# A decoder trunk on one core: the second down pair's parts behind named roundings, and thirteen second-pass pairs by seven products with six of their units kept as whole forms

## The chip, the cores and the metric

The kernel runs on one core of a Trainium2 chip. The metric is the device time of one execution in microseconds. The core has a matmul engine (TensorE, PE in the profile, its weight loads PEld), a vector engine (VectorE, DVE), a scalar engine (ScalarE, ACT), a general engine (GpSimd, POOL) and a queue engine (SyncE, SP). Each engine works through its own list in order. Transfers between the chip's memory (DRAM) and the working memory are issued on SP's or POOL's queue and carried out by 16 DMA engines.

## The reference

The reference is a trunk of two layers on 256 tokens of width 2048, all in 32-bit floats. With the attention cut down to its call, a layer is

```python
for l in range(DEPTH):                                  # DEPTH = 2
    h = _rmsnorm(x, attn_norm_g[l])
    q, k, v, gate_b, gate_c, conv_in = jnp.split(h @ w_in[l], splits, axis=-1)
    ...                                                 # differential attention; short convolution
    x = x + jnp.concatenate([attn, conv], axis=-1) @ w_out[l]
    hm = _rmsnorm(x, mlp_norm_g[l]) @ w_up[l]           # 2048 -> 8192
    x = x + jnp.square(jax.nn.relu(hm)) @ w_down[l]     # 8192 -> 2048
```

The change lies in the last two lines, the MLP.

## The kernel before

**Two parts for each number.** TensorE multiplies a rounded 32-bit form. To keep the precision, each operand is split into a high part (ScalarE copies it into the rounded form) and a low part (VectorE subtracts the high part from the original, and rounds the rest). A product is then three matmuls, high by high, high by low and low by high (`TERMS`). So each weight that is loaded costs ScalarE one pass and VectorE one pass before TensorE may use it. `halves`, `column` and `parts` do this for the different weights.

**The MLP's stages.** The 8192 hidden values are taken as 32 pairs of 128 (`NP`). A pair's up projection gives a tile `h` of blocks A11, A12, A21, A22, each 128 by 128: two halves of the hidden pair by two halves of the tokens. The down projection of a pair is thus a product of a 2 by 2 grid of blocks with a 2 by 2 grid of weight blocks of 128 by 512. There are two ways to do it:

- plain: eight block products, 24 matmuls (line 1142 in the second pass). The weights of a pair are loaded as 1 MB (`raw`) and rounded in two steps of 128 by 1024 (`rows`, line 308).
- by seven products, the scheme of Strassen and Winograd, 21 matmuls (`product`, line 983). It needs sums of the blocks on both sides. On the hidden side these are S1 to S4 (`square`, lines 960 to 963). On the weights' side `quarters` makes three groups of forms: `plain` (the blocks b1 and b2, rounded), `sums` (the tile t of differences, its first half rounded as t13) and `more` (t's second half, rounded as t24). The buffers of b2 and t13 are single; b1 and t24 have two; t has one.

**First pass.** For each pair i TensorE does the up projection (line 937) and, `LAG` = 2 pairs behind, the seven products of pair i - 2 with the left half of the output columns. The rounded form of the pair (`f`, made by `rounded`, two buffers) is used for that. The last two pairs go plain (line 1062). Every pair is also stored in DRAM for the second pass: a pair that is plain there as its rounded form (`plain`, line 969), a pair that goes by seven products there as the unrounded `h` with its sums, 448 KB (`hid`, line 965).

**Second pass.** The same pairs times the right half of the columns. `SEVEN` names the pairs that go by seven products. Such a pair's unit is loaded again into a tile `h` on SP's queue (`load_again`) and rounded again (`unit`, line 975, 128 by 896). Plain pairs come back as blocks of two (`block`, POOL's queue, four buffers). After the last pair of `SEVEN` its products are added into the output (`shared`); after the last plain pair come the rest, and in layer 1 the stores.

**What sets the order.** TensorE's list is in the order of the program. The lists of the other engines are laid out by a planner, which simulates the program's timeline when the kernel is built and may take an instruction earlier than the program names it. Three helpers bind it: `late(ins)` keeps an instruction in program order, `behind(a, b)` lets what is issued within it come only after the given instructions on their engines, and a priority block moves instructions ahead. Weights are made up to `AHEAD` = 3 jobs ahead of TensorE's use, in a list (`weights.order`) that `mlp` writes out; in the second pass the jobs of a seven-product pair are spread among the jobs of the plain pairs before it.

The first down pairs of a layer are a special case. Pair 0's three groups of forms are made during the out projection, behind the roundings that `EARLY_FORMS` names. Pair 1's groups are kept in program order (`keep = late if i == 1`), so they come where TensorE's list reaches them. From pair 2 on the planner places them. `ahead.splits` is the list of the out projection's roundings, one ScalarE and one VectorE instruction each. `split_gained` rounds the normalized activations in the same two steps (lines 275 and 276); `Norm.chunk` calls it for each quarter of the width.

Of the kernel before, what the change touches and what calls it, by code (L numbers as in the profile page):

```python
# [9 lines left out]
F32 = mybir.dt.float32  # L10
F32R = mybir.dt.float32r
AF = mybir.ActivationFunctionType
ALU = mybir.AluOpType
AX = mybir.AxisListType

P = 128
DEPTH = 2
D = 2048
S = 256
# [11 lines left out]
KG = 4  # L31
# [1 line left out]
AHEAD = 3  # L33
NP = DFF // (2 * P)
LAG = 2
SEVEN = (4, 6, 8, 11, 13, 15, 17, 19, 22, 24, 26, 28)
PLAIN = tuple(i for i in range(NP) if i not in SEVEN)

OUT_JOBS = D // P // 2 * (D // CH)
# [68 lines left out]
def trunk(ctx: ExitStack, tc: tile.TileContext, x, w_in, w_out, conv_w, q_norm_g, k_norm_g,  # L108
          lambda_q1, lambda_k1, lambda_q2, lambda_k2, subln_g, attn_norm_g, mlp_norm_g,
          w_up, w_down, rel_bias, selector, out):  # L110
    nc = tc.nc
# [7 lines left out]
    dram = ctx.enter_context(tc.tile_pool(name="dram", bufs=1, space=bass.MemoryType.DRAM))  # L119
# [8 lines left out]
    def behind(*instructions):  # L128

        stack = ExitStack()  # L130
        for ins in instructions:
            stack.enter_context(tc.issue_after(ins.ins))
        return stack

    def bank(name):
        return ps.tile([P, CH], F32, tag="bank", name=name)
# [43 lines left out]
    def norm_gain(which, l, k):  # L180
        i = l * (D // P) + k
        return gains[:, MG + i:MG + i + 1] if which else ngains[:, i:i + 1]
# [89 lines left out]

    def split_gained(dst, k, src, gain, keep=lambda ins: None):

        keep(nc.scalar.activation(dst[:, 0, k], src, AF.Copy, scale=gain))
        keep(nc.vector.scalar_tensor_tensor(
            dst[:, 1, k], src, gain, dst[:, 0, k].bitcast(F32), op0=ALU.mult, op1=ALU.subtract))

    class Parts:

# [158 lines left out]
    class Norm:  # L439
# [9 lines left out]
        def chunk(self, n, wait, banks=None):  # L449
            yield wait  # L450
            a = self.tiles[n].open()
            for j in range(2):
                tp = banks[j] if banks else bank(f"tpn{n}_{j}")
                for i in range(2):
                    k = 2 * j + i
                    for t in range(NT):
                        nc.tensor.transpose(
                            tp[:, i * S + t * P:i * S + (t + 1) * P],
                            xs[n][:, t, k * P:(k + 1) * P], ident)
                with tc.high_priority() if self.which and n == D // CH - 1 else ExitStack():  # L460
                    for i in range(2):
                        k = 2 * j + i
                        split_gained(a, k, tp[:, i * S:(i + 1) * S],
                                     norm_gain(self.which, self.l, n * KG + k))
                self.tiles[n].ready = 2 * j + 2
            self.squares(n)

# [290 lines left out]
    def mlp(l, mnorm, ahead, last):  # L758
# [3 lines left out]
        with ExitStack() as scope:  # L762
            upool = scope.enter_context(tc.tile_pool(name="upool", bufs=3))
            fpool = scope.enter_context(tc.tile_pool(name="fpool", bufs=2))
# [4 lines left out]
            def tile_of(tag, shape, dtype, *rooms):  # L769
                n = turn[tag] = turn.get(tag, -1) + 1  # L770
                pool, tag_in = rooms[max(n - (tag == "draw"), 0) % len(rooms)]
                return pool.tile(shape, dtype, tag=tag_in, name=tag, bufs=1)
# [37 lines left out]
            def quarters(i, col=0):  # L810


                keep = late if i == (SEVEN[0] if col else 1) else lambda ins: None

                def parts(src, tag, bufs):
                    hi, lo = (tile_of(tag + p, list(src.shape), F32R,
                                      *((r, tag + p) for r in (first, second)[:bufs]))
                              for p in "hl")
                    keep(nc.scalar.activation(hi, src, AF.Copy))  # L819
                    keep(nc.vector.tensor_sub(lo, src, hi.bitcast(F32)))  # L820
                    return hi, lo

                def plain():
                    raw = forms["raw"] = load_rows(i, col).rearrange("p k (n c) -> p k n c", n=2)
                    h1, l1 = parts(raw[:, 0, 0], "b1", 2)
                    h2, l2 = parts(raw[:, 1], "b2", 1)
                    return (h1, l1), (h2[:, 0], l2[:, 0]), (h2[:, 1], l2[:, 1])

                def sums():
                    raw = forms["raw"]  # L830
                    t = forms["t"] = first.tile([P, 4, CH], F32, tag="t", name="t")

                    keep(nc.vector.tensor_sub(t[:, 0:2], raw[:, :, 1], raw[:, 0]))  # L833
                    h, lw = parts(t[:, 0:2], "t13", 1)

                    keep(nc.vector.tensor_add(t[:, 2], t[:, 1], raw[:, 0, 0]))
                    keep(nc.vector.tensor_sub(t[:, 3], raw[:, 1, 0], t[:, 2]))  # L837
                    return (h[:, 0], lw[:, 0]), (h[:, 1], lw[:, 1])

                def more():  # L840
                    h, lw = parts(forms["t"][:, 2:4], "t24", 2)
                    return (h[:, 0], lw[:, 0]), (h[:, 1], lw[:, 1])

                if i == 0 and col == 0:
                    made = []
                    for make, job in zip((plain, sums, more), EARLY_FORMS):
                        with behind(*ahead.splits[job - OUT_JOBS]):
                            made.append(make())
                    return tuple(lambda n=n: made[n] for n in range(3))
                return plain, sums, more  # L850

            def rows(i, k, box, col=0):
# [19 lines left out]
            for i in range(NP - LAG, NP):  # L872
# [3 lines left out]

            hid = {i: dram.tile([P, 7 * P], F32, name=f"hid{l}_{i}") for i in SEVEN}
            plain = [dram.tile([P, 2, 2, 4, P], F32R, name=f"plain{l}_{b}")  # L880
                     for b in range(len(PLAIN) // 2)]
            again = {}

            def load_again(i):
                again[i] = tile_of("h", [P, 8, P], F32, (fpool, "h"), (second, "h"))
                nc.sync.dma_start(again[i][:, 1:].rearrange("p a c -> p (a c)"), hid[i])

            def unit(i):
                def make():
                    f = rounded(again[i], 1, 8)  # L890
                    later = SEVEN.index(i) + 1
                    if later < len(SEVEN):
                        load_again(SEVEN[later])
                    return f
                return make
# [54 lines left out]
            def square(i, h):  # L950


                u = h[:, 0:4].rearrange("p a c -> p (a c)")
                nc.scalar.activation(u, u, AF.Relu)
                top = h[:, 0:4].rearrange("p (k t) c -> p k t c", t=2)[:, :, 0]
                nc.vector.tensor_mul(top, top,
                                     mnorm.ratio.unsqueeze(1).to_broadcast([P, 2, P]))
                nc.scalar.activation(u, u, AF.Square)
                if i < NP - LAG:
                    nc.vector.tensor_add(h[:, S1], h[:, A21], h[:, A22])  # L960
                    nc.vector.tensor_sub(h[:, S2], h[:, S1], h[:, A11])
                    nc.vector.tensor_sub(h[:, S3], h[:, A11], h[:, A21])
                    nc.vector.tensor_sub(h[:, S4], h[:, A12], h[:, S2])
                if i in hid:
                    nc.gpsimd.dma_start(hid[i], h[:, 1:].rearrange("p a c -> p (a c)"))
                    return rounded(h, 1, 8)
                f = rounded(h, 0, 8 if i < NP - LAG else 4)
                b = PLAIN.index(i)
                stored.append(nc.gpsimd.dma_start(plain[b // 2][:, b % 2], f[:, :, :4]))
                return f  # L970

            def rounded(h, lo, hi):
                f = fpool.tile([P, 2, 8, P], F32R, tag="f", name="f")
                nc.scalar.activation(f[:, 0, lo:hi], h[:, lo:hi], AF.Copy)  # L974
                nc.vector.tensor_sub(f[:, 1, lo:hi], h[:, lo:hi], f[:, 0, lo:hi].bitcast(F32))  # L975
                return f
# [10 lines left out]
            for i in range(NP):  # L987
                j = i - LAG
                end = i == NP - 1
                h = tile_of("h", [P, 8, P], F32, (fpool, "h"), (second, "h"))  # L990
# [39 lines left out]

            def block(b):
                blocks[b] = apool.tile([P, 2, 2, 4, P], F32R, tag="a", name="g")
                for s in range(2):
                    nc.gpsimd.dma_start(blocks[b][:, s], plain[b][:, s])

            block(0)

            def onto(dst, p, base):
# [15 lines left out]
            sums = shared(*left)  # L1054

            prods[8] = ps.tile([P, CH], F32, tag="av", name=f"pr{l}8", bufs=1)
            for j in range(NP - LAG, NP):
                for k in range(2):
                    b = weights.take()
# [25 lines left out]
            for i in range(NP):  # L1085
                if i in SEVEN:
                    f = weights.take()
# [26 lines left out]
                b, slot = divmod(PLAIN.index(i), 2)  # L1114
# [7 lines left out]
                if i == PLAIN[-1]:  # L1122
                    both = [weights.take() for k in range(2)]
# [34 lines left out]
    for l in range(DEPTH):  # L1158
        mnorm, ahead = mixer(l, norm, first_loads if l == 0 else lambda weights: None)
# [33 lines left out]
```

## Time and profile before

| | |
|---|---|
| median of 3 runs | 2151.32 us (2151.31 to 2152.33) |
| the profiled execution, its own time | 2150.28 us |
| its span, first to last instruction | 2148.5 us |
| granted TensorE clock, mean | 0.999 |
| TensorE busy | 2132.9 us, 10962 matmuls |
| VectorE busy | 1691.0 us |
| ScalarE busy | 1300.1 us |
| DMA | 477.05 MB |

In the profiled execution layer 0's first pass runs from about 393 to 912 us and its second pass to 1081 us; layer 1's first pass from about 1461 to 1978 us and its second pass to the end. A row of the profile names the line, the engine, what is written from what, and the shape; `upc` is the up projection's bank, `pr` the banks of the first pass's products, `rt` those of the second pass, `g` a block of plain pairs, `draw` and `raw` the weights as loaded. A busy TensorE is not TensorE at its peak, since the matmuls overlap; the distance from the start of one matmul to the start of the next is the better measure of its pace.

### The profile page before, as it was taken

What the parts mean: (1) busy time and instruction counts of PE and PEld (TensorE: products, weight loads), DVE (VectorE), ACT (ScalarE), POOL (GpSimd) and SP (SyncE); (2) the same over time, 40 slices, a digit from 0 to 9 for tenths busy, and PEclk for the clock granted to TensorE, in tenths of its full rate; (3) what the DMA queues carried; (4) which work ended last, traced back from release to release, by engine and by line L of the source; (5) the groups of instructions that cost most, each with busy time, mean ns of one, the idle gap of its engine ahead of it and who ended that gap; (6) DMA issues with size and microseconds to landing.
All of it is one profiled execution on the core that took longest, in us unless ns stands there. A gap on an engine that the chain in (4) does not pass through costs nothing.

```text
span 2148.5 us, 28991 instructions
## 1 busy us (share of the span) xinstructions
PE 2132.9 (99%) x10962; PEld 1811.2 (84%) x10962; DVE 1691.0 (79%) x2307; ACT 1300.1 (61%) x1767; POOL 166.0 (8%) x253
## 2 busy tenths in 40 slices
PE   9999999999999999999999999999999999999999
PEld 7888888878888888888888888888788888888887
DVE  6667656688888888799766776566988888887996
ACT  6556445566666666656565664455666666665563
POOL 1021200000000000100001221000000000001000
PEclk9999999999999999999999999999999999999999
DMA  7655668567777777798456556675777777778982
GB/s 257 186 159 165 185 206 264 178 217 230 225 231 234 225 233 225 250 367 308 167 175 177 157 167 186 218 243 187 234 227 231 226 230 233 226 231 277 366 304 76
DMA packets 288245, 477.05 MB, mean 222 GB/s; under 512 B 10689, under 2 KB 191592, under 8 KB 288104
## 3 DMA queue, kind: packets, MB, share of 16 engines
q1 hardware_dynamic: 268104, 417.73, 61.6%
q0 software_dynamic: 19680, 57.18, 8.1%
q8 instruction: 86, 1.41, 0.3%
q14 instruction: 55, 0.45, 0.1%
q10 hardware_dynamic: 320, 0.28, 0.0%
HBM read 441.04 MB, written 34.10 MB: 221 GB/s over the span
## 4 chain that ended last, share of the span: by engine, by line
PE 95%; DVE 3%; ACT 1%; issue 1%; DMA 0%; POOL 0%; SPq 0%; DVEq 0%; ACTq 0%
PE upc L937 31%; PE pr L983 13%; PE rt L1142 9%; PE o L392 8%; PE rt L983 5%; PE ci L414 4%; PE gc L414 4%; PE gb L414 4%; PE v L392 4%; PE q L392 4%; PE k L392 3%; PE upw L937 1%; PE up L937 1%; PE pr L1062 1%; DVE wlo L308 1%
## 5 line engine op out<-in xcount | busy, mean ns | idle before, releaser
L308 DVE TENSOR_TENSOR wlo<-raw,whi 128x1024 fp32r<-128x1024 f32 x328 | 403.4, 1231 | 244.8 <-ACT whi L307 239.4
L307 ACT ACTIVATE whi<-raw 128x1024 fp32r<-128x1024 f32 x328 | 347.0, 1059 | 409.0 <-PE rt L1142 82.7
L937 PE MATMUL upc<-nT,uhi 128*128 128x512 f32 x1920 | 479.0, 392 | 0.0
L795 ACT ACTIVATE uhi<-uraw 128x1024 fp32r<-128x1024 f32 x256 | 270.5, 1057 | 261.7 <-PE upc L937 231.2
L796 DVE TENSOR_TENSOR ulo<-uraw,uhi 128x1024 fp32r<-128x1024 f32 x256 | 313.3, 1224 | 125.7 <-ACT uhi L795 114.6
L937 PEld LDWEIGHTS upc<-nT,uhi 128*128 128x128 f32 x1920 | 353.6, 189 | 68.6
L937 PEld LDWEIGHTS upc<-nT,ulo 128*128 128x128 f32 x1920 | 262.2, 191 | 18.8
L937 PE MATMUL upc<-nT,ulo 128*128 128x256 f32 x1920 | 267.8, 282 | 0.0
L1142 PE MATMUL rt<-whi,g 128*128 128x512 f32 x608 | 191.9, 389 | 0.0
L392 PE MATMUL o<-whi,cat 128*128 128x512 f32 x512 | 159.5, 390 | 0.0
L1142 PEld LDWEIGHTS rt<-whi,g 128*128 128x128 f32 x608 | 114.1, 188 | 23.4
L1142 PE MATMUL rt<-wlo,g 128*128 128x512 f32 x304 | 118.7, 391 | 0.3 <-DVE wlo L308 0.3
L392 PEld LDWEIGHTS o<-whi,cat 128*128 128x128 f32 x512 | 96.2, 188 | 19.7
L820 DVE TENSOR_TENSOR t13l<-t,t13h 128x1024 fp32r<-128x1024 f32 x84 | 102.8, 1223 | 2.1
L820 DVE TENSOR_TENSOR t24l<-t,t24h 128x1024 fp32r<-128x1024 f32 x84 | 102.5, 1221 | 2.2 <-ACT t24h L819 2.2
L819 ACT ACTIVATE t24h<-t 128x1024 fp32r<-128x1024 f32 x84 | 88.7, 1055 | 24.4 <-DVE t L837 24.4
L820 DVE TENSOR_TENSOR b2l<-draw,b2h 128x1024 fp32r<-128x1024 f32 x84 | 102.5, 1220 | 0.5 <-ACT b2h L819 0.5
L833 DVE TENSOR_TENSOR t<-draw 128x1024 f32<-128x1024 f32 x84 | 102.5, 1220 | 0.1
L975 DVE TENSOR_TENSOR f<-h,f 128x896 fp32r<-128x896 f32 (+2 forms) x88 | 98.8, 1123 | 2.5 <-ACT f L974 2.4
L392 PE MATMUL o<-wlo,cat 128*128 128x512 f32 x256 | 99.6, 389 | 0.0
L983 PE MATMUL pr<-t13h,f 128*128 128x512 f32 x240 | 94.0, 392 | 1.6 <-ACT t13h L819 1.6
L819 ACT ACTIVATE t13h<-t 128x1024 fp32r<-128x1024 f32 x84 | 89.1, 1060 | 8.4 <-DVE t L833 3.7
(357 smaller groups left out, 3834.7 us busy)
## 6 DMA issues: line engine op xcount, KB each, us to landing
uraw<-in_w_up_dram SPq DMA_DIRECT2D x128, 1024.0 KB, 5.9
raw<-in_w_in_dram SPq DMA_DIRECT2D x190, 512.0 KB, 4.2
draw<-in_w_down_dram SPq DMA_DIRECT2D x88, 1024.0 KB, 6.0
raw<-in_w_down_dram SPq DMA_DIRECT2D x40, 1024.0 KB, 13.3
raw<-in_w_out_dram SPq DMA_DIRECT2D x64, 512.0 KB, 4.9
plain<-f POOLq DMA_DIRECT2D x40, 512.0 KB, 3.8
g<-plain POOLq DMA_DIRECT2D x40, 512.0 KB, 9.3
hid<-h POOLq DMA_DIRECT2D x24, 448.0 KB, 6.2
```

What stands on the lines that cost most here:

```text
L307: self.splits.append((nc.scalar.activation(hi, raw, AF.Copy), nc.vector.tensor_sub(lo, raw, hi.bitcast(F32))))
L308: nc.vector.tensor_sub(lo, raw, hi.bitcast(F32))))
L392: nc.tensor.matmul(acc[:, t], a.ap[:, pa, k % KG, t * P:(t + 1) * P], (hi, lo)[pw][:, j], start=(k == 0 and n == 0), stop=(k == nk - 1 and ...
L414: nc.tensor.matmul(acc[:, f, 0] if part else acc[:, f], wt[:, k % 4, fs], a.ap[:, 0, k % KG] if part else a.ap[:, :, k % KG], start=(part ...
L795: nc.scalar.activation(hi, src, AF.Copy)
L796: nc.vector.tensor_sub(lo, src, hi.bitcast(F32))
L819: keep(nc.scalar.activation(hi, src, AF.Copy))
L820: keep(nc.vector.tensor_sub(lo, src, hi.bitcast(F32)))
L833: keep(nc.vector.tensor_sub(t[:, 0:2], raw[:, :, 1], raw[:, 0]))
L937: nc.tensor.matmul(acc[:, 0] if part else acc, wt[:, k], a.ap[:, 0, k % KG] if part else a.ap[:, :, k % KG], start=(part == 0 and kh == 0 ...
L983: nc.tensor.matmul(prods[n], f[:, pa, a], b[pw], start=(start and m == 0), stop=(stop and m == 2))
L1142: nc.tensor.matmul(prods[p], blocks[b][:, slot, pa, 2 * k + t], w[pw][:, n], start=(i == PLAIN[0] and k == 0 and m == 0), stop=False)
```

## The change

There are two edits in one diff.

1. **Pair 1's forms.** They are no longer held in program order. Instead `sums` is issued behind the out projection's last rounding (`ahead.splits[-1]`), and `plain` and `more` behind `mnorm.mark`, the last rounding of the MLP's norm. For this `split_gained` returns its two instructions, and `Norm.chunk` keeps the latest of them. The first seven-product pair of the second pass stays in program order as before.
2. **The second pass.** `SEVEN` has thirteen pairs instead of twelve, at other places, so 19 pairs are plain and the last block holds one. Every second pair of `SEVEN` (6, 10, 15, 19, 23, 27) is in `WHOLE`: the first pass stores its rounded form, high and low parts, 896 KB (`both`), and the second pass loads that form straight into an `f` buffer, on POOL's queue, without rounding it again. The other seven are stored and rounded as before.

```diff
-SEVEN = (4, 6, 8, 11, 13, 15, 17, 19, 22, 24, 26, 28)
+SEVEN = (4, 6, 8, 10, 12, 15, 17, 19, 21, 23, 25, 27, 29)
+WHOLE = SEVEN[1::2]
...
     def split_gained(dst, k, src, gain, keep=lambda ins: None):
...
+        return hi, lo
...
-                        split_gained(a, k, tp[:, i * S:(i + 1) * S],
-                                     norm_gain(self.which, self.l, n * KG + k))
+                        self.mark = split_gained(
+                            a, k, tp[:, i * S:(i + 1) * S], norm_gain(self.which, self.l, n * KG + k))
...
-                keep = late if i == (SEVEN[0] if col else 1) else lambda ins: None
+                keep = late if i == SEVEN[0] and col else lambda ins: None
...
+                if i == 1 and not col:
+
+                    def behind_last(make):
+                        def run():
+                            with behind(*(ahead.splits[-1] if make is sums else mnorm.mark)):
+                                return make()
+                        return run
+                    return tuple(behind_last(make) for make in (plain, sums, more))
...
+            both = {i: dram.tile([P, 2, 7, P], F32R, name=f"both{l}_{i}") for i in WHOLE}
             plain = [dram.tile([P, 2, 2, 4, P], F32R, name=f"plain{l}_{b}")
-                     for b in range(len(PLAIN) // 2)]
+                     for b in range((len(PLAIN) + 1) // 2)]
...
             def load_again(i):
+                if i in WHOLE:
+                    f = again[i] = fpool.tile([P, 2, 8, P], F32R, tag="f", name="f")
+                    nc.gpsimd.dma_start(f[:, :, 1:], both[i])
+                    return
...
-                    f = rounded(again[i], 1, 8)
+                    f = again[i] if i in WHOLE else rounded(again[i], 1, 8)
...
                 if i in hid:
                     nc.gpsimd.dma_start(hid[i], h[:, 1:].rearrange("p a c -> p (a c)"))
-                    return rounded(h, 1, 8)
+                if i in SEVEN:
+                    f = rounded(h, 1, 8)
+                    if i in WHOLE:
+                        nc.gpsimd.dma_start(both[i], f[:, :, 1:])
+                    return f
```

More of the change, by code (lines that the diff above doesn't have):

```diff
@@ L273, in split_gained @@
     def split_gained(dst, k, src, gain, keep=lambda ins: None):
-        keep(nc.scalar.activation(dst[:, 0, k], src, AF.Copy, scale=gain))
-        keep(nc.vector.scalar_tensor_tensor(
-            dst[:, 1, k], src, gain, dst[:, 0, k].bitcast(F32), op0=ALU.mult, op1=ALU.subtract))
+        hi = nc.scalar.activation(dst[:, 0, k], src, AF.Copy, scale=gain)
+        keep(hi)
+        lo = nc.vector.scalar_tensor_tensor(
+            dst[:, 1, k], src, gain, dst[:, 0, k].bitcast(F32), op0=ALU.mult, op1=ALU.subtract)
+        keep(lo)
+        return hi, lo
     class Parts:
@@ L875, in mlp @@
                 rows(i, 1, box)
-            hid = {i: dram.tile([P, 7 * P], F32, name=f"hid{l}_{i}") for i in SEVEN}
+            hid = {i: dram.tile([P, 7 * P], F32, name=f"hid{l}_{i}") for i in SEVEN
+                   if i not in WHOLE}
+            both = {i: dram.tile([P, 2, 7, P], F32R, name=f"both{l}_{i}") for i in WHOLE}
             plain = [dram.tile([P, 2, 2, 4, P], F32R, name=f"plain{l}_{b}")
-                     for b in range(len(PLAIN) // 2)]
+                     for b in range((len(PLAIN) + 1) // 2)]
             again = {}
             def load_again(i):
+                if i in WHOLE:
+                    f = again[i] = fpool.tile([P, 2, 8, P], F32R, tag="f", name="f")
+                    nc.gpsimd.dma_start(f[:, :, 1:], both[i])
+                    return
                 again[i] = tile_of("h", [P, 8, P], F32, (fpool, "h"), (second, "h"))
@@ L1032, in block @@
                 blocks[b] = apool.tile([P, 2, 2, 4, P], F32R, tag="a", name="g")
-                for s in range(2):
+                for s in range(min(2, len(PLAIN) - 2 * b)):
                     nc.gpsimd.dma_start(blocks[b][:, s], plain[b][:, s])
```

## The prediction

> **What bounds the kernel now.** I read the page first: busy times and the chain that ended last.
>
> ```profile
> span 2148.5 us, 28991 instructions
> ...
> PE 2132.9 (99%) x10962; PEld 1811.2 (84%) x10962; DVE 1691.0 (79%) x2307; ACT 1300.1 (61%) x1767; POOL 166.0 (8%) x253
> ...
> PE 95%; DVE 3%; ACT 1%; issue 1%; DMA 0%; POOL 0%; SPq 0%; DVEq 0%; ACTq 0%
> ```
>
> TensorE sets the end: 95% of the chain is its own work. So an edit can pay in two ways, by fewer matmuls or by taking away one of the few moments in which TensorE waits. The waits of TensorE alone come next (columns: total us, times, longest).
>
> ```profile
> PE pr L983 <- DVE t13l L820: 3.2, 2, 1.6
> PE pr L983 <- ACT t13h L819: 1.6, 2, 0.8
> ...
> PE pr L983 <- DVE b2l L820: 0.3, 2, 0.2
> PE rt L1142 <- DVE wlo L308: 0.3, 2, 0.2
> ```
>
> The largest are all of one kind: a product of the first pass (L983 writing `pr`) waits for the rounded parts of a down pair, twice, so once in each layer. The timeline of TensorE shows where, and what it costs (columns: start, us, matmul, count, idle before).
>
> ```profile
> 438.89 0.39 PE L983 MATMUL pr<-b1h,f 128*128 128x512 f32 x1
> ...
> 442.82 0.51 PE L983 MATMUL pr<-t13h,f 128*128 128x512 f32 x1 [0.78 <-ACT t13h L819]
> 444.94 0.50 PE L983 MATMUL pr<-t13l,f 128*128 128x512 f32 x1 [1.61 <-DVE t13l L820]
> ...
> 445.51 3.49 PE L937 MATMUL upc<-nT,uhi 128*128 128x512 f32 x8
> ...
> 452.67 0.40 PE L983 MATMUL pr<-t13h,f 128*128 128x512 f32 x1
> ```
>
> ```profile
> 1506.55 0.39 PE L983 MATMUL pr<-b1h,f 128*128 128x512 f32 x1
> ...
> 1513.17 2.00 PE L937 MATMUL upc<-nT,uhi 128*128 128x512 f32 x8
> ...
> 1518.75 0.40 PE L983 MATMUL pr<-t13h,f 128*128 128x512 f32 x1
> ...
> 1526.37 0.40 PE L983 MATMUL pr<-b1h,f 128*128 128x512 f32 x1
> ...
> 1529.12 1.98 PE L937 MATMUL upc<-nT,uhi 128*128 128x512 f32 x8
> ```
>
> These are the products of down pair 1, the second one. Its first twelve matmuls take 445.51 - 438.89 = 6.62 us, and 1513.17 - 1506.55 = 6.62 us in layer 1. The same twelve of pair 2 take 1529.12 - 1526.37 = 2.75 us. Each layer therefore loses 3.87 us here, more than the wait rows add up to, since the pipeline also refills. In layer 0 the up matmuls behind the stall then need 452.67 - 445.51 = 7.16 us where layer 1 needs 1518.75 - 1513.17 = 5.58 us: another 1.58 us. The granted clock explains it (stretch of 8 us: busy us and count of PE, PEld, DVE, ACT, POOL, then clock, DMA share, GB/s).
>
> ```profile
> 445.00:453.00 8.00, 8.00 (x36) 6.76 (x37) 6.41 (x7) 3.20 (x4) 0.00 (x0) 0.79 0.41 136
> ```
>
> Together the stall costs 3.87 + 3.87 + 1.58 = 9.32 us.
>
> **Edit 1: pair 1's parts behind named roundings.** It adds no instruction and removes none. Today pair 1's `quarters` are held in program order (`keep = late`), so VectorE reaches them only when TensorE already wants them:
>
> ```profile
> 438.72 0.68 DVE L820 TENSOR_TENSOR b1l<-draw,b1h 128x512 fp32r<-128x512 f32 x1
> 439.32 1.22 DVE L820 TENSOR_TENSOR b2l<-draw,b2h 128x1024 fp32r<-128x1024 f32 x1
> 440.45 1.22 DVE L833 TENSOR_TENSOR t<-draw 128x1024 f32<-128x1024 f32 x1
> ...
> 443.66 1.22 DVE L820 TENSOR_TENSOR t13l<-t,t13h 128x1024 fp32r<-128x1024 f32 x1
> ```
>
> After the edit the planner may put them anywhere behind the last rounding of the out projection (`sums`) or behind the last split of the MLP norm (`plain`, `more`). Three things limit how early: the raw rows, the single buffers of `b2` and `t13`, and room on VectorE. Their rows:
>
> ```profile
> 362.39 0.46 SPq L805 DMA_DIRECT2D draw<-in_w_down_dram  x1
> ```
>
> ```profile
> 424.80 0.39 PE L983 MATMUL pr<-b2h,f 128*128 128x512 f32 x1
> ...
> 431.74 0.39 PE L983 MATMUL pr<-t13h,f 128*128 128x512 f32 x1
> ```
>
> ```profile
> 392.00:438.00 46.00, 45.25 (x253) 39.16 (x252) 30.58 (x53) 27.79 (x40) 2.41 (x4) 1.00 0.73 229
> ```
>
> The raw rows of pair 1 are asked for at 362.39, some 75 us before use. Pair 0's last read of `b2` starts at 424.80 and of `t13` at 431.74. From there to the need at 438.89 and, nine matmuls of 0.23 us on, about 441, there are 14 and 9 us for parts of 1.22 us on VectorE and their first halves on ScalarE. VectorE is idle for 46.00 - 30.58 = 15.4 us between 392 and 438. The work to be moved, by the rows above and the groups below, is b1l 0.69 + b2l 1.22 + t 1.22 + two halves 1.37 + t13l 1.22 + t24l 1.22 = 6.94 us. It fits, and it hides under TensorE's up matmuls. If that room did not serve, the cost would be what it is now.
>
> What is late next? Pair 2's parts will be wanted 3.87 us earlier (5.45 in layer 0), but they stand behind 6.94 us of VectorE work that has moved forward. So I take the whole 9.32 us; the bounds are 0 (nothing moves) and 9.32. Nor is a loss excluded: a `t13` rounding put on ScalarE's in-order queue before 431.74 would hold the `uhi` roundings behind it, and TensorE would wait for those.
>
> The clock term is the softest. [...]
>
> **Edit 2: thirteen pairs by seven products, six units whole.** TensorE's price per pair in the second pass (seven-product pair 4, plain pair 5, pair 6):
>
> ```profile
> 934.13 0.39 PE L983 MATMUL rt<-b1h,f 128*128 128x512 f32 x1
> ...
> 938.89 0.39 PE L1142 MATMUL rt<-whi,g 128*128 128x512 f32 x1
> ...
> 944.34 0.39 PE L983 MATMUL rt<-b1h,f 128*128 128x512 f32 x1
> ...
> 949.10 0.39 PE L1142 MATMUL rt<-whi,g 128*128 128x512 f32 x1
> ```
>
> Seven products (21 matmuls) take 4.76 us, a plain pair (24) takes 5.45 us. One more pair per layer turned into seven products saves 0.69 us, 1.38 us in both layers.
>
> The cover for this is VectorE, which has little left in that pass:
>
> ```profile
> 938.00:970.00 32.00, 32.00 (x143) 26.50 (x142) 31.86 (x34) 20.53 (x22) 1.05 (x2) 1.00 0.93 330
> ```
>
> ```profile
> L308 DVE TENSOR_TENSOR wlo<-raw,whi 128x1024 fp32r<-128x1024 f32 x328 | 403.4, 1231 | 244.8 <-ACT whi L307 239.4 <-PE ci L414 3.4
> ...
> L820 DVE TENSOR_TENSOR t13l<-t,t13h 128x1024 fp32r<-128x1024 f32 x84 | 102.8, 1223 | 2.1
> ...
> L837 DVE TENSOR_TENSOR t<-draw,t 128x512 f32<-128x512 f32 x84 | 57.7, 687 | 0.6
> ...
> L820 DVE TENSOR_TENSOR b1l<-draw,b1h 128x512 fp32r<-128x512 f32 x84 | 57.6, 686 | 0.0
> ...
> L975 DVE TENSOR_TENSOR f<-h,f 128x896 fp32r<-128x896 f32 x48 | 52.2, 1087 | 0.1
> ```
>
> A plain pair costs VectorE 2 x 1.23 = 2.46 us, a seven-product pair 6.94 us and its unit's rounding 1.09 us. Per layer that is 12 x 8.03 + 20 x 2.46 = 145.6 us now and 13 x 6.94 + 7 x 1.09 + 19 x 2.46 = 144.6 us after: the six units kept whole pay for the thirteenth pair, with 1 us over. So I put VectorE at nothing. Without them it would be 151.1 us, and since the stretch above is full, the extra would come out as waits like the one on `wlo`.
>
> What the whole units add is bytes and a queue. Each is stored from `f` and loaded again as 896 KB instead of 448 KB, and the load goes from SP's queue to POOL's:
>
> ```profile
> raw<-in_w_down_dram SPq DMA_DIRECT2D x17, 1024.0 KB, 13.3
> ...
> g<-plain POOLq DMA_DIRECT2D x18, 512.0 KB, 9.3
> h<-hid SPq DMA_DIRECT2D x11, 448.0 KB, 3.9
> ```
>
> The load needs the `f` buffer of two seven-product pairs before. For pair 10 that is pair 6, which ends at 949.10 in the rows above; pairs 7, 8 and 9 lie between, so 5.45 + 4.76 + 5.45 = 15.66 us are left. Pairs 19, 23 and 27 have the same 15.66 us, pair 15 one plain pair more, pair 6 the start of the pass: four tight loads per layer. No row shows an 896 KB load on POOL. The bounds are 2 x 3.9 = 7.8 us (by `hid`) and 9.3 x 896 / 512 = 16.3 us (by `g`). I take 13.3 x 896 / 1024 = 11.6 us, by the row nearest in size and stage: hidden, cost 0. The upper bound gives 0.6 us x 8 = 5 us of waits. Behind the waiting load stand the `g` blocks of later plain pairs, which have four buffers, two pairs in each, and can stand it. The larger stores of the first pass are read out of `f`, which is wanted again two pairs later (1526.37 - 1506.55, less the stall, is 15.95 us a pair): 0. The seven-product run now ends one pair nearer the layer's end, so the sums into the right half meet the last roundings of weights: 0, bounds 0 to 1 us per layer.
>
> **The sum.** 9.32 + 1.38 = 10.70 us. The profiled execution took 2150.28 us, so 2139.6 us; the median of the runs is 2151.32 us, 1.04 us above it, and carrying that over gives 2140.6 us.
>
> **The rivals.** *The stall moves to pair 2.* VectorE is busy after the stall too (6.41 of 8 us in the clock's row), and now TensorE gives it no pause. If half of the 9.32 us comes back as waits on pair 2's or 3's parts, the time is 2151.32 - 4.66 - 1.38 = 2145.3 us. Against it: no wait on a later pair's parts in the whole first pass.
>
> *The parts stay where they are.* The planner's own clock decides where a part goes; if it holds the move for useless, only edit 2 is left: 2149.9 us. Against it: the parts of pairs from 2 on aren't held, and TensorE never waits for them.
>
> *Slower: the whole units come late.* The tight loads on POOL's queue can't start before TensorE lets `f` go, and they share a nearly full DMA (share 0.93 above) with the raw loads. For it speaks the longest landing of a `g` load around the second pass of layer 0:
>
> ```profile
> DMA to landing us min/median/max: 4.3/9.1/19.7
> ```
>
> At 19.7 us each of eight loads is 4.0 us late: +32 us, 2172.9 us. It decides from 15.66 + 10.70 / 8 = 17.0 us on, and a mean landing of 16.3 us would leave 2145.6 us. Against it: the load stands first in its queue when its buffer comes free, and 9.1 us is the median of loads issued two at a time.
>
> **Chances.** Forecast 0.62 (2137.5 to 2143, the lower end if both layers lose the clock in the timed runs, 1.58 us more, if the 0.3 us wait on `wlo` goes too, and with the runs' own spread of 1.0 us); stall moves 0.14; parts stay 0.10; late units 0.09, of which a third still ends faster; ScalarE held up, net near zero or slower, 0.05. A measurement of this kernel tells about 0.2%, 4.3 us, from no change: faster is below 2147.0, slower above 2155.6. That gives faster 0.74, same 0.16, slower 0.10. The range 2137.5 to 2150.2 takes in the first three cases.
>
> **What would show it.** Right: the twelve matmuls of pair 1 in 2.75 us in both layers, no granted clock under 1.00 around 445, no TensorE wait on `t13` or `b2`; 10956 matmuls; 40 roundings 896 wide where there are 48, and twelve loads of `f` on POOL, the tight ones landing in under 15.66 us; VectorE's sum in the second pass about unchanged. Wrong: TensorE waits on pair 2's parts or on `uhi` in the first pass, or on `f` at the start of pairs 10, 19, 23 or 27, or new waits within 11 us of a layer's end.

## The result and the profile after

| | before | after |
|---|---|---|
| median | 2151.27 us (2148.07 to 2152.84) | 2145.21 us (2143.91 to 2148.14) |
| ratio, 95% interval | | 0.9976 [0.9967, 0.9985] |
| profiled execution, its span | 2150.28, 2148.5 us | 2145.36, 2143.5 us |

By the ratio the change makes the kernel 0.24% faster, about 5 us; the two medians differ by 6.1 us. The forecast was 10.7 us. The page of after first (span, busy times, chain of waits):

```profile
span 2143.5 us, 28946 instructions
...
PE 2129.0 (99%) x10956; PEld 1811.2 (84%) x10956; DVE 1690.7 (79%) x2307; ACT 1292.7 (60%) x1761; POOL 174.8 (8%) x263
...
PE 95%; DVE 3%; ACT 1%; DMA 1%; issue 1%; POOL 0%; ACTq 0%; DVEq 0%
```

The six matmuls are gone, 10956 instead of 10962, and the shares are as before. The waits of TensorE in after (total us, times, longest) tell more:

```profile
PE rt L1164 <- DVE wlo L312: 4.4, 2, 2.2
```

All waits on `pr`, the first pass's products, have left the list. In their place stands a new one, once per layer, in the second pass: TensorE waits for a low part of a plain pair's weights. TensorE's timeline of after at pair 1 (start, us, matmul, count) shows what edit 1 did:

```profile
438.81 0.40 PE L1005 MATMUL pr<-b1h,f 128*128 128x512 f32 x1
...
440.88 0.39 PE L1005 MATMUL pr<-t13h,f 128*128 128x512 f32 x1
441.11 0.39 PE L1005 MATMUL pr<-t13l,f 128*128 128x512 f32 x1
...
441.56 1.98 PE L955 MATMUL upc<-nT,uhi 128*128 128x512 f32 x8
```

The twelve matmuls take 441.56 - 438.81 = 2.75 us where they took 6.62. The same place in the second pass of after shows the new loss, first layer 0, then layer 1:

```profile
922.29 0.64 PE L1164 MATMUL rt<-whi,g 128*128 128x512 f32 x2
925.14 0.49 PE L1164 MATMUL rt<-wlo,g 128*128 128x512 f32 x1 [2.20 <-DVE wlo L312]
...
926.86 0.62 PE L1164 MATMUL rt<-whi,g 128*128 128x512 f32 x2
```

```profile
1985.65 0.63 PE L1164 MATMUL rt<-whi,g 128*128 128x512 f32 x2
1988.49 0.80 PE L1164 MATMUL rt<-wlo,g 128*128 128x512 f32 x1 [2.21 <-DVE wlo L312]
...
1991.65 0.64 PE L1164 MATMUL rt<-whi,g 128*128 128x512 f32 x2
```

These are the matmuls of pair 3, the last plain pair ahead of the first seven-product pair, pair 4. From the start of the last row before the wait, which holds two matmuls, to the first start behind it are 925.14 - 922.29 = 2.85 us. By the rows at 440.88 and 441.11 two matmuls need 2 x 0.23 us, so 2.39 us are lost. In layer 1 it is 2.38 us, and then seven matmuls need 1991.65 - 1988.49 = 3.16 us instead of 1.59 (7/21 of the 4.76 us that a seven-product pair took), another 1.57 us; in layer 0 they need 926.86 - 925.14 = 1.72 us, 0.13 us more. The granted clock (third number from the end of a stretch's row, ahead of the DMA share and GB/s) had a mean of 0.51 there, and was 1.00 at the same wait of layer 0:

```profile
922.00:927.00 5.00, 2.80 (x13) 1.96 (x12) 4.96 (x6) 2.39 (x3) 0.00 (x0) 1.00 1.08 405
1988.20:1991.70 3.50, 3.21 (x8) 2.53 (x9) 2.67 (x4) 0.00 (x0) 0.00 (x0) 0.51 1.07 406
```

The account of the profiled execution: 9.32 us (first pass, as forecast) and 1.38 us (matmuls) gained; lost 2.39 + 2.38 + 1.57 + 0.13 = 6.47 us. Gone is also a pause at pair 1 of the second pass, here in before:

```profile
1985.76 0.61 PE L1142 MATMUL rt<-whi,g 128*128 128x512 f32 x2
1986.55 0.50 PE L1142 MATMUL rt<-wlo,g 128*128 128x512 f32 x1 [0.17 <-DVE wlo L308]
1986.88 0.63 PE L1142 MATMUL rt<-whi,g 128*128 128x512 f32 x2
```

Three matmuls take 1986.88 - 1985.76 = 1.12 us instead of 0.68 (the three before them, 1985.08 to 1985.76), 0.44 us per layer or 0.88 us. The sum is -9.32 - 1.38 - 0.88 + 6.47 = -5.11 us, and the spans differ by 5.0.

Why pair 3's low part was late is read on ScalarE and VectorE. ScalarE before and after, start of layer 0's second pass:

```profile
922.19 1.06 ACT L819 ACTIVATE t13h<-t 128x1024 fp32r<-128x1024 f32 x1 [1.02 <-DVE t L833]
925.46 2.01 ACT L307 ACTIVATE whi<-raw 128x1024 fp32r<-128x1024 f32 x2 [2.21 <-DMA raw<-in_w_down_dram]
928.42 1.06 ACT L819 ACTIVATE t24h<-t 128x1024 fp32r<-128x1024 f32 x1 [0.94 <-DVE t L837]
```

```profile
915.64 1.06 ACT L823 ACTIVATE t13h<-t 128x1024 fp32r<-128x1024 f32 x1
920.37 1.06 ACT L823 ACTIVATE t24h<-t 128x1024 fp32r<-128x1024 f32 x1 [3.67 <-DVE t L841]
921.34 1.99 ACT L311 ACTIVATE whi<-raw 128x1024 fp32r<-128x1024 f32 x2
```

VectorE before and after, the same stretch:

```profile
926.56 1.23 DVE L308 TENSOR_TENSOR wlo<-raw,whi 128x1024 fp32r<-128x1024 f32 x1 [0.40 <-ACT whi L307]
...
928.30 1.22 DVE L308 TENSOR_TENSOR wlo<-raw,whi 128x1024 fp32r<-128x1024 f32 x1
929.51 1.23 DVE L820 TENSOR_TENSOR t24l<-t,t24h 128x1024 fp32r<-128x1024 f32 x1
```

```profile
919.64 0.69 DVE L841 TENSOR_TENSOR t<-draw,t 128x512 f32<-128x512 f32 x1
921.46 1.23 DVE L824 TENSOR_TENSOR t24l<-t,t24h 128x1024 fp32r<-128x1024 f32 x1 [1.12 <-ACT t24h L823]
922.72 1.22 DVE L837 TENSOR_TENSOR t<-draw 128x1024 f32<-128x1024 f32 x1
923.87 2.35 DVE L312 TENSOR_TENSOR wlo<-raw,whi 128x1024 fp32r<-128x1024 f32 x2
```

Before, pair 3's two `whi` stand ahead of pair 4's `t24h`. After, `t24h` stands first, waits 3.67 us for `t`, and `whi` follows it; on VectorE, where pair 3's `wlo` stood ahead of `t24l` before, they now follow `t24l` and `t` of pair 6. They are begun at 923.87 us; TensorE wanted the first at 922.29 + 2 x 0.23 = 922.75. Nothing needs `t24` before 933.9 us, 11 us later, as TensorE's groups say (lengths in ns, then the first and last start):

```profile
L1005 PE MATMUL rt<-t24h,f x104: 388/389/390, 933.9 to 2127.7; 128*128 128x512 f32 x104
```

### The profile page after: what moved, and what is told of

Its sections match the earlier page's. It is cut to its first block, busy times and chain, and to the rows that moved or that the text cites. A ratio compares the mean times of both kernels' runs of the same rounds, so it can differ in the third digit from the quotient of the medians.

```text
span 2143.5 us, 28946 instructions
## 1 busy us (share of the span) xinstructions
PE 2129.0 (99%) x10956; PEld 1811.2 (84%) x10956; DVE 1690.7 (79%) x2307; ACT 1292.7 (60%) x1761; POOL 174.8 (8%) x263
## 3 DMA queue, kind: packets, MB, share of 16 engines
q8 instruction: 86, 1.41, 0.3%
## 4 chain that ended last, share of the span: by engine, by line
PE 95%; DVE 3%; ACT 1%; DMA 1%; issue 1%; POOL 0%; ACTq 0%; DVEq 0%
PE upc L955 31%; PE pr L1005 13%; PE o L396 8%; PE rt L1164 7%; PE rt L1005 6%; PE ci L418 4%; PE gc L418 4%; PE gb L418 4%; PE v L396 4%; PE q L396 4%; PE k L396 3%; DVE wlo L312 1%; PE upw L955 1%; PE up L955 1%; PE pr L1084 1%
## 5 line engine op out<-in xcount | busy, mean ns | idle before, releaser
L312 DVE TENSOR_TENSOR wlo<-raw,whi 128x1024 fp32r<-128x1024 f32 x324 | 398.1, 1231 | 245.3 <-ACT whi L311 240.0
L1164 PE MATMUL rt<-whi,g 128*128 128x512 f32 x576 | 183.2, 391 | 0.0
L1164 PEld LDWEIGHTS rt<-whi,g 128*128 128x128 f32 x576 | 108.9, 189 | 22.9 <-ACT whi L311 0.3
L1164 PE MATMUL rt<-wlo,g 128*128 128x512 f32 x288 | 113.1, 393 | 4.4 <-DVE wlo L312 4.4
L823 ACT ACTIVATE b2h<-draw 128x1024 fp32r<-128x1024 f32 x86 | 90.4, 1051 | 3.0 <-PE rt L1005 2.2
```

What stands on the lines that cost most here:

```text
L312: nc.vector.tensor_sub(lo, raw, hi.bitcast(F32))))
L1164: nc.tensor.matmul(prods[p], blocks[b][:, slot, pa, 2 * k + t], w[pw][:, n], start=(i == PLAIN[0] and k == 0 and m == 0), stop=False)
```

## The experiments

Before was timed beside each: a median of 2149.77 us for the first four, 2149.87 us for the last four. Theory A: the wait comes from the order that the planner gave the lists, since the removed rounding of pair 6's unit let pair 4's forms move ahead of pair 3's weights. Rival B: it comes from the added bytes of the whole units, which delay the loads of weights.

**Edit 1 alone.** The kernel after, with the old set of pairs and no whole unit.

```diff
-SEVEN = (4, 6, 8, 10, 12, 15, 17, 19, 21, 23, 25, 27, 29)
-WHOLE = SEVEN[1::2]
+SEVEN = (4, 6, 8, 11, 13, 15, 17, 19, 22, 24, 26, 28)
+WHOLE = ()
```

> Edit 1 alone: pair 1's parts behind the named roundings, the twelve old seven-product pairs, no unit kept whole. Theory A (the new wait of the second pass comes from edit 2, which lets ScalarE's list take the t24 form of pair 4 ahead of the roundings of plain pair 3): the first-pass stall is gone, the wait at pair 3 is absent (under 0.5 us a layer, as before), 9.3 us less than before, about 2142.0. Rival B (bytes: the 896 KB load of pair 6 delays the raw rows of pair 3): the same as A here. Rival C (edit 1 itself shifts the vector work into the second pass): the wait of about 2.5 us at pair 3 is here too, about 2147.

Measured: 2140.55 us (2140.16 to 2140.97), ratio 0.9957 [0.9944, 0.9969], 9.2 us less. There is no wait on `pr`, the mean granted clock is 1.000 in all five executions, and the pause on `wlo` at pair 1 of the second pass is where it was. Edit 1 alone gives more than the whole change.

**Edit 2 alone.** The kernel after, with pair 1's groups in program order again.

```diff
-                keep = late if i == SEVEN[0] and col else lambda ins: None
+                keep = late if i == (SEVEN[0] if col else 1) else lambda ins: None
...
-                if i == 1 and not col:
-                    ...
```

> Edit 2 alone: thirteen seven-product pairs, six units whole, pair 1's parts in place as before. Theory A and rival B: the first-pass stall is there (3.87 us a layer), the wait at pair 3 of the second pass is there (2.4 to 2.6 us a layer, less 0.45 of before), and 1.38 us of matmuls are saved: 2.7 us more than before, about 2154, and up to 1.6 us more where a half clock follows a wait. Rival C: no wait at pair 3, about 2149.9.

Measured: 2154.11 us (2150.06 to 2158.02), ratio 1.0019 [1.0010, 1.0028]: slower. TensorE's waits have both losses:

```profile
PE rt L1156 <- DVE wlo L312: 4.4, 2, 2.2
PE pr L997 <- DVE t13l L824: 3.2, 2, 1.6
```

So the new wait belongs to edit 2 and does not need edit 1: -9.2 and +4.3 us add up to -4.9, about what both together gave.

**Pair 6's unit rounded again.** All as after, but the first of the six whole units, that of pair 6, is stored and rounded as before.

```diff
-WHOLE = SEVEN[1::2]
+WHOLE = SEVEN[3::2]
```

> The changed kernel, but pair 6 is stored and rounded as before (five units whole: 10, 15, 19, 23, 27). ScalarE's list then has pair 6's rounding in its old place and pair 3's roundings ahead of pair 4's t24. Theory A and rival B: no wait at pair 3, 10.7 us less than before, about 2140.6. If the six saved roundings were all needed as cover: waits on low parts elsewhere in the second pass, 2142 or more. Rival C: the wait stays, about 2145.

Measured: 2140.07 us (2139.61 to 2141.05), ratio 0.9955 [0.9942, 0.9967]. The wait at pair 3 is gone; what is left on `wlo` are three pauses of 0.2 us by the list of waits (0.34 to 0.40 us by the starts). This fits A, and B too, since pair 6's 448 KB more and its load on POOL's queue are gone as well.

**Pair 4's last group one place later.** The bytes and the queues are those of after. Only the slot of pair 4's `more` group (t24) in the list of weights is moved behind pair 3's.

```diff
-                    mine[0], mine[1], mine[5], mine[3]]
+                    mine[0], mine[1], mine[5], mine[7]]
```

> The changed kernel with one number changed: pair 4's last group of forms (t24) is asked for after pair 3's second rounding instead of after pair 1's. Pair 6 stays whole, so all bytes and queues are those of the changed kernel; only the lists of ScalarE and VectorE have pair 3's roundings ahead of t24. Theory A: no wait at pair 3, 10.7 to 11.6 us less than before, about 2140.2. Rival B: the raw rows of pair 3 are as late as in the changed kernel, the wait of 2.4 us a layer stays, about 2145.

Measured: 2139.14 us (2138.76 to 2139.53), ratio 0.9950 [0.9938, 0.9963]. ScalarE's, VectorE's and GpSimd's timelines and the row of the waits:

```profile
919.52 2.01 ACT L311 ACTIVATE whi<-raw 128x1024 fp32r<-128x1024 f32 x2 [3.32 <-PE rt L1164]
921.43 1.04 ACT L823 ACTIVATE t24h<-t 128x1024 fp32r<-128x1024 f32 x1
```

```profile
920.62 2.36 DVE L312 TENSOR_TENSOR wlo<-raw,whi 128x1024 fp32r<-128x1024 f32 x2 [0.78 <-ACT whi L311]
```

```profile
906.17 0.71 POOL L901 DMA_DIRECT2D f<-both  x1 [3.23 <-PE pr L1084]
```

```profile
PE rt L1164 <- DVE wlo L312: 0.2, 1, 0.2
```

`whi` is again ahead of `t24h`, and starts at 919.52 us instead of 921.34. Pair 6's unit is loaded as in after (906.17 us here, 906.66 there), so the same bytes are in flight; `whi` waited for TensorE to free its buffer and not for a load. So pair 3's weights had landed in time with all the bytes of after, and the wait is gone: the bytes alone don't make it. The row also shows that most of the 3.67 us for which ScalarE stood idle in after were not the loss, since `whi` itself has 3.32 us to wait here. Beside edit 1 alone this kernel is 1.41 us faster; the prediction put 1.38 us on the six matmuls.

**No whole unit.** All thirteen pairs by seven products, every unit rounded again. This takes the cover away with which the prediction paid for the thirteenth pair.

```diff
-WHOLE = SEVEN[1::2]
+WHOLE = ()
```

> The changed kernel with no unit kept whole: thirteen seven-product pairs, all units stored and rounded as before the change. The lists have pair 3's roundings ahead of pair 4's t24. If the second pass needs the six saved roundings as cover (VectorE full there, as the prediction had it): up to 6.5 us a layer of new waits on low parts, 2144 to 2152. If VectorE only looks full because it works ahead: as the changed kernel without its wait, 2139.5 to 2141.

Measured: 2139.19 us (2138.37 to 2139.52), ratio 0.9947 [0.9935, 0.9960], as fast as the kernel before it. VectorE in the second pass, 928 to 1058 us (layer 0), in before, in after and without whole units, and last the stretch that the prediction called full, without whole units:

```profile
928.00:1058.00 130.00, 130.00 (x575) 107.65 (x574) 116.92 (x117) 78.08 (x83) 5.28 (x10) 1.00 0.76 272
```

```profile
928.00:1058.00 130.00, 130.00 (x575) 107.71 (x574) 114.72 (x114) 75.71 (x80) 8.35 (x14) 1.00 0.78 275
```

```profile
928.00:1058.00 130.00, 130.00 (x575) 107.70 (x574) 121.72 (x123) 80.77 (x87) 4.77 (x9) 1.00 0.72 252
...
938.00:970.00 32.00, 32.00 (x143) 26.51 (x142) 31.90 (x34) 19.91 (x23) 1.58 (x3) 1.00 0.87 296
```

VectorE works 4.8 us more in these 130 us than in before, is full from 938 to 970 us, and TensorE doesn't wait once in them. So VectorE was not the bound there. It had 130 - 117 = 13 us to spare in before; that it looks full in the 32 us because it works ahead fits this, but no run tests it apart.

**Extra bytes.** Pair 6 rounded as in the third experiment, and beside it a copy of 1 MB from DRAM to DRAM on POOL's queue, written into the program at the place of pair 6's load. Its data isn't used.

```diff
+                if i == SEVEN[1]:
+                    spill = dram.tile([P, 2, 2, 4, P], F32R, name=f"spill{l}")
+                    nc.gpsimd.dma_start(spill, plain[0])
```

> As e3 (pair 6 rounded as before, five units whole), but where the changed kernel asks for pair 6's 896 KB on POOL's queue, 1 MB is copied within DRAM on the same queue, read and used by nobody. Theory A (the wait comes from the lists, and the lists change because pair 6's rounding is gone): lists as in e3, no wait at pair 3, 2140 to 2141. Rival B (bytes at the start of the pass): wait on the low part of pair 3, 2 us a layer or more, 2144 and up.

Measured: 2139.73 us (2138.95 to 2140.16), ratio 0.9950 [0.9937, 0.9962], and no wait at pair 3. But the copy didn't run where it was written:

```profile
433.84 0.53 POOL L905 DMA_DIRECT2D spill<-plain  x1 [5.14 <-DMA plain<-f]
```

It started at 433.84 us (1495.1 us in layer 1), in the first pass, as soon as the block that it reads had been stored; pair 6's load starts at 906.66 us in after. It put no byte into the start of the second pass, so this run repeats the third experiment and says nothing about B.

**The order alone.** Edit 1 alone, with pair 3's first roundings issued behind pair 4's `t24` by force; beside edit 1 alone no unit, byte or pair is changed. The lines against after, without those of edit 1 alone:

```diff
+                def kept(ins):
+                    late(ins)
+                    last_parts.append(ins)
...
-                    return weights.halves(...)
+                    with behind(*(last_parts[-2:] if col and i == 3 and k == 0 else ())):
+                        return weights.halves(...)
```

> Edit 1 alone, as e1 (twelve old pairs, no whole unit), plus one constraint: the roundings of pair 3's first weights in the second pass are issued behind pair 4's t24 roundings, on ScalarE and on VectorE. No byte and no instruction differs from e1. Theory A: this order alone makes the wait at pair 3, 2.0 to 2.5 us a layer, 4 to 5 us over e1, more in executions where a half clock follows: 2144.5 to 2147. Rival B: as e1, 2140.6.

Measured: 2143.53 us (2142.86 to 2143.86), ratio 0.9967 [0.9955, 0.9979], 3.0 us over edit 1 alone. So the order makes a wait without any of the whole units' bytes, but a smaller one than expected. The rows of ScalarE and VectorE, and TensorE's wait behind them:

```profile
921.14 1.06 ACT L828 ACTIVATE t24h<-t 128x1024 fp32r<-128x1024 f32 x1 [3.67 <-DVE t L846]
922.11 1.99 ACT L311 ACTIVATE whi<-raw 128x1024 fp32r<-128x1024 f32 x2
```

```profile
922.23 1.23 DVE L829 TENSOR_TENSOR t24l<-t,t24h 128x1024 fp32r<-128x1024 f32 x1 [1.13 <-ACT t24h L828]
923.38 1.22 DVE L312 TENSOR_TENSOR wlo<-raw,whi 128x1024 fp32r<-128x1024 f32 x1
```

```profile
922.70 1.00 PE L1170 MATMUL rt<-whi,g 128*128 128x512 f32 x2
924.65 0.50 PE L1170 MATMUL rt<-wlo,g 128*128 128x512 f32 x1 [0.95 <-DVE wlo L312]
```

In after, pair 6's `t` (1.22 us, at 922.72) stood between `t24l` and the first `wlo`; here it doesn't, and the loss is 924.65 - 922.70 - 2 x 0.23 = 1.49 us per layer instead of 2.4. How much each instruction costs can be estimated. With pair 4's group one place later, `wlo` waited for `whi` alone and started 920.62 - 919.52 = 1.10 us behind it. By that distance it could have started at 922.11 + 1.10 = 923.21 here and started at 923.38, so about 1.3 of the 1.49 us come from `t24h` standing ahead of `whi` on ScalarE, and 0.17 from `t24l` on VectorE. In after it could have started at 921.34 + 1.10 = 922.44 and started at 923.87: of the 2.39 us about 1.0 come from `t24h` on ScalarE, 0.3 from `t24l` and 1.1 from pair 6's `t` on VectorE. No run takes away one of the three alone. All six executions ran at a mean granted clock of 1.000, so none shows a half clock behind the wait. Here the order makes a wait without the bytes, and in the experiment on pair 4's last group all the bytes are there without the wait: B falls.

**Fourteen pairs.** The change carried on: pairs 3, 5, ... 29 by seven products, seven units whole.

```diff
-SEVEN = (4, 6, 8, 10, 12, 15, 17, 19, 21, 23, 25, 27, 29)
+SEVEN = tuple(range(3, 30, 2))
...
-                    mine[0], mine[1], mine[5], mine[3]]
+                    mine[0], mine[1], mine[3], mine[5]]
```

> Fourteen pairs by seven products (3, 5, ... 29), seven units whole, the forms of the first one spread over pairs 0 to 2. If the start of the second pass had room: 3 matmuls a layer fewer than e4, 1.4 us less, 2137.8. Theory A says that the start of the pass is where VectorE and ScalarE have no room and any list that puts forms ahead of plain weights is paid in waits: waits on low parts in pairs 0 to 5, 2140 or more.

Measured: 2143.07 us (2140.57 to 2144.01), ratio 0.9964 [0.9952, 0.9977], slower than thirteen pairs with the order put right. The waits that theory A named for the start of the pass did not come: `rt` waits for no `wlo` in the whole execution, so the start of the pass had room for the fourteenth pair. TensorE has one long wait, at the end of layer 0, and ScalarE's timeline says for what:

```profile
PE rt L1149 <- DVE x L1061: 3.7, 1, 3.7
```

```profile
1069.68 1.06 ACT L311 ACTIVATE whi<-raw 128x1024 fp32r<-128x1024 f32 x1 [3.56 <-DMA raw<-in_w_in_dram]
```

ScalarE waited 3.56 us for a weight of the next layer's attention to land; on VectorE that weight's `wlo` (from 1070.77 us) stands ahead of the sum `x` (from 1071.91) for which TensorE waited until 1072.71. Why this load was late was not looked into. The one execution at a mean granted clock of 1.000 took 2140.57 us, the other four, at 0.998 and 0.999, 2142.71 us or more.

## Why the prediction was wrong, step by step

- **Edit 1, 9.32 us: right.** Edit 1 alone measured 9.2 us. The twelve matmuls take the 2.75 us named for them. What the prediction called the pipeline's refilling is measured in before: at the `t13l` wait the matmul behind it took 0.50 us instead of 0.39, and the next one started 445.27 - 444.94 = 0.33 us behind it instead of 0.23. VectorE's timeline of after shows where the parts went: `b1` and `t24` right behind the norm, `b2` behind pair 0's read at 424.80, `t13` behind that at 431.74:

```profile
401.61 0.68 DVE L824 TENSOR_TENSOR b1l<-draw,b1h 128x512 fp32r<-128x512 f32 x1
402.21 1.22 DVE L824 TENSOR_TENSOR t24l<-t,t24h 128x1024 fp32r<-128x1024 f32 x1
```

```profile
426.24 1.23 DVE L824 TENSOR_TENSOR b2l<-draw,b2h 128x1024 fp32r<-128x1024 f32 x1
...
433.18 1.23 DVE L824 TENSOR_TENSOR t13l<-t,t13h 128x1024 fp32r<-128x1024 f32 x1
```

  Pair 2 didn't become late, and the rivals "stall moves to pair 2", "parts stay" and "ScalarE held up" all fall.
- **The clock term, 1.58 us: right in size for the profiled execution, soft as said.** Beside the experiments, executions of before at a mean granted clock of 1.000 took 2148.2 to 2148.9 us, those at 0.998 took 2150.95 to 2152.51 us. At 1.000 edit 1 alone gains about 8 us, the 7.74 us of the stall itself.
- **The matmuls, 1.38 us: right.** Six fewer are counted, and a seven-product pair takes 4.76 us in after too (pair 4, 930.50 to 935.26). The 1.41 us between edit 1 alone and the kernel with pair 4's group later agree with it, but so closely only by luck: the other kernels with thirteen pairs and no wait at pair 3 lie 0.48, 0.82 and 1.36 us below edit 1 alone, and each kernel's own executions spread by 0.8 to 1.4 us.
- **"I put VectorE at nothing": the step that failed.** The sum of work was right: over the whole execution VectorE is busy for 1690.7 us where it was 1691.0, and between 928 and 1058 us for 2.2 us less. But putting its cost at nothing on that sum left out the order of the lists, and that is what the edit changed; "What is late next?" was asked for edit 1 only. Taking out pair 6's rounding (1.09 us at 916.99 us of before) at the start of the pass, and moving its load, gave the planner another order, in which pair 4's `t24` (on ScalarE and VectorE) and pair 6's `t` (on VectorE) come ahead of pair 3's weights. In after `t24h` on ScalarE waited 3.67 us for `t`, and `whi` behind it started at 921.34 us; with `whi` ahead (pair 4's last group one place later) it started at 919.52. So roundings that nobody wanted yet made needed ones late: 2.4 us per layer, and in layer 1 a granted clock of 0.51 in the 3.50 us around its end. The runs show that the order alone makes a wait (2 x 1.5 us with `t24` in the way; in after, with pair 6's `t` as well, it is 2 x 2.4), that rounding pair 6 again or moving one slot takes it away, and that it is gone with all the bytes of after in flight. Whether the missing rounding or the moved load turned the planner's choice was not separated.
- **The cover: wrong.** The prediction said that without the whole units "the extra would come out as waits like the one on `wlo`"; it did not. It took a stretch of 32 us in which VectorE is full for the load of the pass. VectorE had 13 us in 130 to spare. The kernel without whole units is as fast as the best with six, so they bought nothing, and pair 6's brought the wait.
- **The whole units' loads: hidden as forecast, their duration too long.** The line that loads them, for the five loads behind pair 6's in layer 0:

```profile
L901 POOL DMA_DIRECT2D f<-both x5: 703/703/721, 945.9 to 1033.0; - x5
...
DMA to landing us min/median/max: 5.0/7.9/8.3
```

  At most 8.3 us, and 9.8 us in layer 1, where 11.6 was taken and 7.8 was the lower bound; 15.66 us were there. Pair 6's own load, beside the first weights of the pass, landed in 20.4 and 18.1 us, above the upper bound of 16.3, but it was asked for at 906.66 us, pair 6's products come some 34 us later, and TensorE never waits for an `f`. The rival "whole units late" falls. The roundings 896 wide number 40, as named.
- **The layer's end, 0 to 1 us: right** for thirteen pairs (the wait of `rt` on `x` there is 0.4 us before and after); with fourteen it cost 3.7 us.
- **The range:** that after lies inside 2137.5 to 2150.2 us is luck, since its cause was not among the rivals named. So is that the rival "stall moves to pair 2" gave 2145.3 us, next to the 2145.21 measured: its waits aren't there. The list of what would show it wrong had waits on `f`, on pair 2's parts and at the layer's end; pair 3's weights at the start of the second pass were not in it.

Both the kernel with pair 4's group one place later (2139.14 us) and the one without whole units (2139.19 us) beat before and after. The second is the simpler.

## What to carry to other kernels

An edit that takes work off an engine can still make TensorE wait (2.4 us per layer here), where a planner lays out the engines' lists: look at which instruction moves up, what stands behind it, and when that is wanted. A stretch in which an engine is full doesn't show that the engine is the bound (VectorE was busy for 31.90 of 32 us without whole units, TensorE for all 32); add up its work over the whole stage, and look whether TensorE waits there. Test two edits of one diff apart: here one gave 9.2 us and the other took 4.3 of them back. And look in the trace where an added instruction ran before its run is used as evidence: the extra copy ran 470 us ahead of the place where it was written.

## What the runs showed of the hardware

Half clock followed some short waits and not others. In after the equal waits of 2.2 us in both layers were followed by half clock in layer 1 alone: in steps of 0.5 us from 1988.20 to 1991.70 us the clock is 0.54, five times 0.50 and 0.54, and 1.00 in the steps on either side. It lasted 3.4 us: the row of 3.50 us at a mean of 0.51 gives 3.50 x (1 - 0.51) x 2 = 3.4, and the prediction's row of before, 8.00 us at 0.79, gives 3.4 as well. By an estimate from these rows half clock for 3.4 us costs half of it, 1.7 us; the matmuls there took 1.57 us more in after and 1.58 us more in before. In edit 1 alone with the order forced, waits of 0.95 us left the mean at 1.000. One kernel's time differs with the mean granted clock from one execution to the next: edit 2 alone took 2150.06 us in its one execution at a mean granted clock of 1.000, 2153.01 us in one at 0.999, 2153.9 to 2154.8 us in eight at 0.998, and 2158.02 us in one at 0.996. The six kernels of the experiments in which no wait of TensorE is over 1.0 us kept a mean of 1.000 in every execution and spread by 0.8 to 1.4 us, where after spread by 4.2 us. By an estimate from edit 2 alone, which has two such stalls per layer, a stall removed is worth its own length and up to (2158.02 - 2150.06) / 4 = 2.0 us more.
